# Background steps at even rates, the second block's tokens loaded at once, masks for two chunks, and last results further apart

## The chip, the cores and the metric

The kernel runs on one core of a Trainium2 chip. The time is device time of one launch in microseconds (us), as the median of several runs. A profile of one execution says when each engine worked: TensorE (PE, with its weight loads as PEld), VectorE (DVE), ScalarE (ACT), GpSimd (POOL) and SyncE (SP), which issues nearly all the transfers.

## The reference

One layer of a diffusion backbone in float32: 1024 latent tokens and 256 context tokens of 1024 channels, one sample. What is computed, cut short:

```
m = silu(c) @ w_ada + b_ada                 # 9 chunks of 1024: shift, scale, gate of three sublayers
h = x   + 0.5 * gate * rmsnorm(swiglu(modulate(rmsnorm(x)), w13_a, w2_a))     # latent, and so the context
p = modulate(rmsnorm(h)) @ w_in + b_in      # Fourier input, q, k, v, o, head gates, branch gates
h_l = bidirectional chunkwise mLSTM(q, k, v, gates; state from the context), 4 heads, 8 chunks of 128 tokens
  #   per chunk and direction: w = exp(dmat - m_t) where the triangle allows, s = (q k^T) * w
y = sigmoid(g_f) * (fft3(xf) @ w_four) + sigmoid(g_m) * (sigmoid(o) * rmsnorm(h_l) @ w_mproj)
h = h + gate * rmsnorm(y @ w_out)
out = h + 0.5 * gate * rmsnorm(swiglu(modulate(rmsnorm(h)), w13_b, w2_b))     # 22 row blocks of 128 in w2
```

## The kernel before

**Products.** Every float32 product of size is three matmuls (`mm3`, line 172): each operand is split into a rounded high part and the rest, and high x high, high x low and low x high are summed. So weights must be loaded (tile `wr`), cast by ScalarE to `wh`, and the difference taken by VectorE into `wl`, before TensorE can use them. `wunit` (lines 141 and 142) does that for a unit of 1024 columns; `split_act` (164 and 165) for others. There are three buffers each of `wr`, `wh` and `wl`. The large products over the 1024 latent tokens, seen as two blocks of 512, use Winograd's seven products of half-size blocks in place of eight: `ffn_in` and `mix_pairs` for the wide projections, `wino_out` for the two output products of the feed-forwards (order n = 1, 6, 7, 4, 5, 3, 2, with operands `gx` from memory; `done` adds and stores a finished column), `mix_values` for the values.

**Stages,** in order of time: modulation and the first block's normalisation; first feed-forward (`ffn_in`, then `wino_out` to 741 us); the context's feed-forward (`ffn_ctx_in`, `ffn_ctx_out`, to 930 us); head gates; the Fourier input's columns for block 1, then block 0 (`fourier_cols`, four units of weights each); pairs of q, k and gates (`mix_pairs`); values (`mix_values`); the context's projections and states; the mLSTM of four heads between projections of gates (1423 to 1789 us); the merge; second feed-forward, with its output product from 2454 us.

**Background work.** All work of other engines that isn't tied to the running product (normalisations, residuals, sums of blocks, modulation chunks, head steps) is written as generators that stop after each small step. Between the matmuls, `tick(part)` is called; it adds `rate * part` to a credit of at most 8 and runs one step for each whole credit. Credit that was left from before is spent at once. `later` appends generators and sets the rate; `drain` runs all that is left; `side` is a second such line of steps with its own rate:

```
        self.credit = min(self.credit + self.rate * part, 8.0)
        while self.bg and self.credit >= 1.0:
```

So rates and credit decide the order in which instructions stand in each engine's queue, and each queue runs in order. Nothing else orders the work; the tile framework adds the semaphores.

**Names that the change touches.** `load_x` loads tokens (tile `o` or `g`), squares them on ScalarE, transposes them and writes `xT`; for the second block it runs as a background generator, two row tiles at a step. `spill` writes the first block's tiles to `xT`. `second` makes the second block's operands. `enter` makes the operands of the mix, `combos` and `combos_rest` their sums over blocks. `mix_pairs` prepares weights of a pair in stages (`upto`): raw loads, sums on POOL, casts. `ada_rest` loads w_ada in tiles of 128 x 512 and sums them with the conditioning vector on VectorE (line 286), two loads ahead; in the mLSTM it is the side job, for chunks 5 to 8 of the modulation. In `mlstm_head`, `weigh` turns the log weights of a chunk into weights (adds a column and the mask on VectorE, exponential on ScalarE), and `scores` makes the products with q. `final` normalises and stores the last results, a column of 128 tokens at a time and a half of its 1024 channels; when the second half is there, its result is written.

Of the kernel before, what the change touches and what calls it, by code (L numbers as in the profile page):

```python
# [35 lines left out]
class Kernel:  # L36
# [349 lines left out]
    def load_x(self, src, T, name, out, keep=False, tag="o"):  # L386
# [6 lines left out]
        for j0 in range(0, n, 2):  # L393
            xs = {}
            for j in range(2):
                for hf in range(2):
                    x = xs[j, hf] = self.s512("g" if keep else tag)
                    r = (j0 + j) * P
                    nc.sync.dma_start(x, src[r : r + P, hf * TB : (hf + 1) * TB])
                    junk = self.s512("b" if tag == "o" else tag)  # L400
                    q = 2 * (j0 + j) + hf
                    nc.scalar.activation(junk, x, AF.Square, accum_out=ssq[:, q : q + 1])
                yield
# [73 lines left out]
    def operands(self, tiles, rstd, u, s, i, out):  # L477
# [10 lines left out]
        for k in range(4):  # L488
# [9 lines left out]
            nc.gpsimd.tensor_tensor(u1, uh[k].bitcast(F32), ul[k].bitcast(F32), op=ALU.add)  # L498
            nc.gpsimd.tensor_tensor(u2, uh[k + 4].bitcast(F32), ul[k + 4].bitcast(F32), op=ALU.add)
# [268 lines left out]
    def wino_out(self, w2, gx, tokens, done):  # L768
# [65 lines left out]
        for n in (1, 6, 7, 4, 5, 3, 2):  # L834
# [4 lines left out]
            for s in steps:  # L839
# [3 lines left out]
                if n == 2 and s[-1] in steps[-2]:  # L843
# [373 lines left out]
    def ctx_project(self, u, gw):  # L1217
# [46 lines left out]
        for c in range(2):  # L1264
# [4 lines left out]
            self.later(self.ctx_states((2 * c, 2 * c + 1), kt, va, gates), rate=3.0)  # L1269
# [122 lines left out]
    def mix_pairs(self, U, gates):  # L1392
# [29 lines left out]
        upto(0, "raw")  # L1422
        upto(0, 3)
# [116 lines left out]
    def mlstm_head(self, h, q, k, v, gates):  # L1540
# [50 lines left out]
        def weigh(c):  # L1591

            for d in range(2):
                nc.vector.scalar_tensor_tensor(W(c)[:, d, :], W(c)[:, d, :], col(3, c, d), self.mask[:, d, :],
                                               op0=ALU.add, op1=ALU.add)
            nc.scalar.activation(W(c), W(c), AF.Exp)

        def scores(c):
# [26 lines left out]
            nc.vector.tensor_scalar_mul(pr, SW[:, 1, :], rd[:, 1:2])
            nc.vector.scalar_tensor_tensor(pr, SW[:, 0, :], rd[:, 0:1], pr, op0=ALU.mult, op1=ALU.add)
# [62 lines left out]
    def fourier_cols(self, u2, b, units):  # L1689
# [459 lines left out]
```

## Time and profile before

| | us |
|---|---|
| median of 3 runs (2695.95 to 2700.22) | 2696.79 |
| the profiled execution | 2690.76 |
| its span in the trace | 2689.0 |
| TensorE busy | 2607.1 |
| VectorE busy | 1943.2 |
| ScalarE busy | 1157.7 |
| GpSimd busy | 248.7 |

The granted TensorE clock is 0.992 of full speed as a mean, and the transfers move 186 GB/s as a mean. The span runs from the first to the last instruction; the time holds 1.8 us more around it. Busy time of an engine is a sum over stages, so what limits a stage is read in windows of that stage. In a list of waits a row names who waited (engine, tile written, line), for what it waited last, and the total, number and longest of those waits.

### The profile page before, as it was taken

How to read it: one execution, taken by the hardware profiler on the slowest of the kernel's cores; microseconds unless marked ns; L12 is line 12 of the kernel's file. 1: busy time of each engine (PE TensorE's matmuls, PEld its weight loads, DVE VectorE, ACT ScalarE, POOL GpSimd, SP SyncE). 2: the span in 40 equal slices, each digit the busy share in tenths (PEclk: the TensorE clock that was granted, in tenths of full speed). 3: DMA queues.
4: the chain of work that ended last, by engine and by line, in shares of the span. 5: the costliest groups of instructions: out<-in, count | busy, mean ns of one | idle time of the engine just before them, and what ended most of it. 6: DMA issues, size and time to landing. Idle time of an engine off the chain costs nothing.

```text
span 2689.0 us, 34491 instructions
## 1 busy us (share of the span) xinstructions
PE 2607.1 (97%) x11497; PEld 2080.0 (77%) x11497; DVE 1943.2 (72%) x3493; ACT 1157.7 (43%) x2003; POOL 248.7 (9%) x380
## 2 busy tenths in 40 slices
PE   8999999999999999999999999999999999999998
PEld 5778888777777768887777777878887788888876
DVE  5688787899788748866856666656658787865665
ACT  4543333454455435542543443433345433334542
POOL 1111011000000023210000000000002010111000
PEclk9999999999999999999999999999999999999999
DMA  8765454868586642345665654456546554537774
GB/s 297 251 200 176 149 169 156 285 220 292 164 260 217 180 139 90 114 133 161 185 201 180 187 162 128 149 159 214 175 136 218 182 168 153 175 111 265 244 255 137
DMA packets 421978, 499.92 MB, mean 186 GB/s; under 512 B 27137, under 2 KB 258218, under 8 KB 421800
## 3 DMA queue, kind: packets, MB, share of 16 engines
q1 hardware_dynamic: 406728, 451.06, 53.7%
q0 software_dynamic: 14928, 46.59, 4.6%
q8 instruction: 91, 1.49, 0.2%
q14 instruction: 87, 0.71, 0.1%
q10 hardware_dynamic: 144, 0.07, 0.0%
HBM read 387.58 MB, written 110.04 MB: 185 GB/s over the span
## 4 chain that ended last, share of the span: by engine, by line
PE 74%; DVE 10%; DMA 8%; issue 5%; ACT 2%; SPq 1%; POOL 1%; DVEq 0%; POOLq 0%; ACTq 0%
PE mm L172 66%; DMA ld<-in_w_ada_dram 2%; DMA wr<-in_w_a_dram 2%; PE qc L1611 1%; DVE wl L142 1%; PE mm L1210 1%; DVE u L286 1%; DMA ld<-xT 1%; DMA ld<-h 1%; DVE b L441 1%; DMA t<-r_l 1%; PE aux L1762 1%; ACT wh L141 1%; PE mm L263 1%; DMA ld<-xT_c 0%
## 5 line engine op out<-in xcount | busy, mean ns | idle before, releaser
L172 PE MATMUL mm<-g,wh 128*128 128x512 f32 (+1 forms) x2112 | 686.8, 406 | 4.8 <-DVE m L1972 2.4
L172 PE MATMUL mm<-g,o 128*128 128x512 f32 x2352 | 555.9, 394 | 0.0
L172 PEld LDWEIGHTS mm<-g,o 128*128 128x128 f32 x2352 | 441.8, 188 | 103.9
L172 PEld LDWEIGHTS mm<-g,wh 128*128 128x128 f32 (+1 forms) x2112 | 389.9, 188 | 92.5 <-issue 3.8
L172 PE MATMUL mm<-g,wl 128*128 128x512 f32 (+1 forms) x1056 | 415.9, 395 | 0.0
L142 DVE TENSOR_TENSOR wl<-wr,wh 128x1024 fp32r<-128x1024 f32 x190 | 232.7, 1226 | 95.8 <-ACT wh L141 94.1
L172 PE MATMUL mm<-wh,g 128*128 128x512 f32 x920 | 295.3, 397 | 4.9 <-ACT wh L141 3.4
L141 ACT CAST wh<-wr 128x1024 fp32r<-128x1024 f32 x190 | 198.7, 1047 | 229.1 <-PE mm L172 164.8
L172 PE MATMUL mm<-u,wh 128*128 128x512 f32 (+1 forms) x848 | 268.3, 398 | 4.4 <-DVE m L518 2.8
L172 PEld LDWEIGHTS mm<-g,wl 128*128 128x128 f32 (+1 forms) x1056 | 198.6, 188 | 45.0 <-DVE wl L165 0.2
L172 PEld LDWEIGHTS mm<-wh,g 128*128 128x128 f32 x920 | 172.4, 188 | 47.9 <-ACT wh L141 4.7
L172 PE MATMUL mm<-wh,u 128*128 128x512 f32 x608 | 201.9, 406 | 3.9 <-ACT g L442 3.0
L172 PEld LDWEIGHTS mm<-u,wh 128*128 128x128 f32 (+1 forms) x848 | 159.8, 191 | 42.2 <-DVE m L518 3.2
L172 PE MATMUL mm<-wl,g 128*128 128x512 f32 x460 | 182.6, 397 | 0.2
L628 DVE TENSOR_TENSOR t<-mm,t 128x512 f32<-128x512 f32 x148 | 101.8, 688 | 99.6 <-PE mm L172 99.6
L172 PE MATMUL mm<-u,wl 128*128 128x512 f32 (+1 forms) x424 | 167.8, 398 | 2.5 <-DVE wl L142 2.5
L164 ACT CAST wh<-wr 128x1024 fp32r<-128x1024 f32 (+1 forms) x90 | 79.3, 881 | 165.2 <-PE mm L172 92.1
L164 ACT CAST o<-wa 128x512 fp32r<-128x512 f32 x108 | 66.9, 621 | 171.9 <-PE mm L172 165.4
L172 PEld LDWEIGHTS mm<-wh,u 128*128 128x128 f32 x608 | 116.3, 192 | 31.3 <-issue 3.4
L165 DVE TENSOR_TENSOR g<-t,g 128x512 fp32r<-128x512 f32 x156 | 104.5, 687 | 39.2 <-ACT g L164 31.9
L172 PE MATMUL mm<-wl,u 128*128 128x512 f32 x304 | 124.6, 410 | 6.0 <-DVE wl L142 6.0
L164 ACT CAST g<-t 128x512 fp32r<-128x512 f32 x156 | 92.5, 620 | 64.7 <-PE mm L172 46.4
(514 smaller groups left out, 3940.8 us busy)
## 6 DMA issues: line engine op xcount, KB each, us to landing
wr<-in_w_a_dram SPq DMA_DIRECT2D x124, 512.0 KB, 4.5
t<-gx SPq DMA_DIRECT2D x170, 256.0 KB, 4.0
wr<-in_w_b_dram SPq DMA_DIRECT2D x70, 512.0 KB, 4.4
wr<-in_w_in_dram SPq DMA_DIRECT2D x66, 512.0 KB, 4.0
gx<-m POOLq DMA_DIRECT2D x88, 256.0 KB, 3.7
gx<-t POOLq DMA_DIRECT2D x66, 256.0 KB, 3.8
ld<-in_w_ada_dram SPq DMA_DIRECT2D x64, 256.0 KB, 2.8
ld<-h SPq DMA_DIRECT2D x52, 256.0 KB, 3.7
```

The costliest lines, as they stand in the source:

```text
L141: nc.scalar.copy(hv, rv)
L142: nc.vector.tensor_tensor(lv, rv, hv.bitcast(F32), op=ALU.subtract)
L164: self.nc.scalar.copy(hi, src)
L165: self.nc.vector.tensor_tensor(lo, src, hi.bitcast(F32), op=ALU.subtract)
L172: mul = lambda x, y, start, stop: self.nc.tensor.matmul(out, x, y, start=start, stop=stop, skip_group_check=grown)
L263: nc.tensor.matmul(pt[:2, :], self.sc[:, k, :], t, start=k == 0, stop=k == ND - 1)
L286: nc.vector.scalar_tensor_tensor(acc[s], t, self.sc[:, k, s : s + 1], acc[s], op0=ALU.mult, op1=ALU.add)
L441: nc.vector.scalar_tensor_tensor(t, x, sc[:, d : d + 1], rb, op0=ALU.mult, op1=ALU.mult)
L628: add = lambda o, x, y: nc.vector.tensor_tensor(o, x, y, op=ALU.add)
L1210: nc.tensor.matmul(pt[:, :257], kw[:, i * P : (i + 1) * P], vaug, start=True, stop=True)
L1611: nc.tensor.matmul(pt[:, :257], at(q, i, c), C[:, i * 257 : (i + 1) * 257], start=i == 0, stop=i == 1)
L1762: nc.tensor.matmul(pt[:, jj * 256 : (jj + 1) * 256], zz[i][:, j * P : (j + 1) * P], m, start=i == 0, stop=i == 1)
```

## The change

It alters rates, resets credit, and moves instructions; the large products stay the same.

- `later` can set the credit to zero (`fresh`), and `paced` sets the rate when its generator begins.
- Second block's tokens: its loads use the 36 buffers of `g`, two row tiles (four loads) ahead; the first is issued before the feed-forward's weights. `spill` writes four tiles a step. The operands that follow have a rate of 2.8 in place of 5.
- `wino_out`: no background steps in the last three k of n = 5 and n = 3; for n = 2 with tokens as rows, the last three groups of k (and not two) are run together, column by column, so that a column ends every 15 matmuls in place of 9.
- `operands` (lines 498 and 499): the sums u1 and u2 of high and low parts go from POOL to VectorE, twice in each of its four steps' groups.
- `combos` at 0.6 without the credit from before (1.2), `enter` at 1.7 (2.0), and the context's states at 2.4 and then 10 (3), with no credit from before; the normalisations beside `mix_values` at 1.6 (2.0), the last feed-forward's operands at 4.2 (5.0).
- The first pair of `mix_pairs` is prepared at the last two units of `fourier_cols(0)`, not ahead of it.
- mLSTM: the mask is added to two chunks and both directions in one instruction; the column goes into the exponential as a bias, one for each direction; one of the two products of the scores goes to ScalarE. The side job has chunks 5 to 7 at 5.8 in place of 5 to 8 at 7.5.
- Chunk 8 is the side job in the last output product at 2.0, with tiles `u`; the row gains of `final` follow when it is done.

The diff, cut to its core:

```
     def later(self, *gens, rate=1.0, fresh=False):
         self.bg.extend(gens)
         self.rate = rate
+        if fresh:
+            self.credit = 0.0
+    def paced(self, gen, rate):
+        self.rate = rate
+        yield from gen
...
             u1, u2, s1 = self.s512("b"), self.s512("wa"), self.s512("b")
-            nc.gpsimd.tensor_tensor(u1, uh[k].bitcast(F32), ul[k].bitcast(F32), op=ALU.add)
-            nc.gpsimd.tensor_tensor(u2, uh[k + 4].bitcast(F32), ul[k + 4].bitcast(F32), op=ALU.add)
+            nc.vector.tensor_tensor(u1, uh[k].bitcast(F32), ul[k].bitcast(F32), op=ALU.add)
+            nc.vector.tensor_tensor(u2, uh[k + 4].bitcast(F32), ul[k + 4].bitcast(F32), op=ALU.add)
...
-                if n == 2 and s[-1] in steps[-2]:
+                if n == 2 and (s in steps[-3:-1] if tokens else s == steps[-2]):
                     continue
...
-                    self.tick(1 / 8)
+                    if n not in (5, 3) or k < NP - 3:
+                        self.tick(1 / 8)
...
+            if c % 2 == 0:
+                t = decay[c // 2].rearrange("p (d c s) -> p d c s", d=2, c=2)
+                nc.vector.tensor_tensor(t, t, self.mask.unsqueeze(2).to_broadcast([P, 2, 2, P]), op=ALU.add)
             for d in range(2):
-                nc.vector.scalar_tensor_tensor(W(c)[:, d, :], W(c)[:, d, :], col(3, c, d), self.mask[:, d, :],
-                                               op0=ALU.add, op1=ALU.add)
-            nc.scalar.activation(W(c), W(c), AF.Exp)
+                nc.scalar.activation(W(c)[:, d, :], W(c)[:, d, :], AF.Exp, bias=col(3, c, d))
...
-            nc.vector.tensor_scalar_mul(pr, SW[:, 1, :], rd[:, 1:2])
+            nc.scalar.activation(pr, SW[:, 1, :], AF.Copy, scale=rd[:, 1:2])
...
-            self.later(self.spill(xl[0][0], xl[0][2]), self.load_x(block(x, 1), TB, "1", xl[1]), second(), rate=5.0)
+            load = self.load_x(block(x, 1), TB, "1", xl[1], xtag="g")
+            next(load)
+            self.later(self.spill(xl[0][0], xl[0][2]), load, self.paced(second(), 2.8), rate=6.0)
...
-        self.later(enter(1), enter(0), rate=2.0)
+        self.later(enter(1), enter(0), rate=1.7)
...
-        self.later(self.combos(u2, U, held), rate=1.2)
+        self.later(self.paced(self.combos(u2, U, held), 0.6), rate=1.7)
...
-        next(pairs)
-        self.fourier_cols(u2, 0, units)
+        self.fourier_cols(u2, 0, units, lambda: next(pairs))
...
-                self.later(self.prenorm(self.reload(self.h1c, CTX), rc1, CTX, 1, 1, uc), rate=2.0)
+                self.later(self.prenorm(self.reload(self.h1c, CTX), rc1, CTX, 1, 1, uc), rate=1.6, fresh=True)
...
-        self.side, self.side_rate = self.ada_rest([0], [5, 6, 7, 8], ("ld", "acc", "rb", "b"), lag=2), 7.5
+        self.side, self.side_rate = self.ada_rest([0], [5, 6, 7], ("ld", "acc", "rb", "b"), lag=2), 5.8
...
+        self.side, self.side_rate = self.ada_rest([0], [8], "uuuu", lag=2), 2.0
         self.wino_out(w2, gx, True, self.final(h2t))
```

Four places show what moves in the queues. On VectorE, where the context's output product begins (L142 and L150 are the weight differences, L957 and L982 the context's own products, L1324 and L1352 the block sums of `combos`, L443 and L467 `enter`), before:

```order
L957 TENSOR_TENSOR t_7774<-mm_7680,t_7774 128x256
L1324 TENSOR_TENSOR t_7799<-g_7295,g_7303 128x512
L957 TENSOR_TENSOR t_7777<-mm_7681,t_7777 128x256
L1324 TENSOR_TENSOR ld_7801<-g_7299,g_7307 128x512
L1324 TENSOR_TENSOR ld_7803<-g_7468,g_7476 128x512
L142 TENSOR_TENSOR wl_7787<-wr_7784,wh_7786 128x1024
L165 TENSOR_TENSOR wa_7796<-aux_7790,wa_7795 128x512
L1324 TENSOR_TENSOR t_7805<-g_7472,g_7480 128x512
L1324 TENSOR_TENSOR b_7807<-t_7799,ld_7801 128x512
L1324 TENSOR_TENSOR t_7820<-g_7296,g_7304 128x512
L1324 TENSOR_TENSOR t_7799<-ld_7803,t_7799 128x512
```

and after, from the first block sum:

```order
L1352 TENSOR_TENSOR t_7871<-g_7517,g_7525 128x512
L467 SCALAR_TENSOR_TENSOR g_7705<-b_7779,ada_l,g_7697 128x512
L465 SCALAR_TENSOR_TENSOR b_7785<-ld_7759,pre_7540,rb_7717 128x512
L465 SCALAR_TENSOR_TENSOR b_7809<-ld_7783,pre_7540,rb_7717 128x512
L150 TENSOR_TENSOR wl_7860<-wr_7857,wh_7859 128x1024
L467 SCALAR_TENSOR_TENSOR g_7706<-b_7785,ada_l,g_7698 128x512
L150 TENSOR_TENSOR wl_7890<-wr_7887,wh_7889 128x1024
L467 SCALAR_TENSOR_TENSOR g_7707<-b_7809,ada_l,g_7699 128x512
```

The sums of `combos` stood several between two weight differences and now come later, with steps of `enter` in their place.

On SP, in `fourier_cols(0)` (the block's units are `wr` of 128x2x512, the first pair's weights `wr` of 128x8x128 and the tiles of L540 or L564; L1706 and L1736 store the results of the block before), before:

```order
L540 DMA ld_8654<-in_w_in_dram 128x4x128
L127 DMA wr_8619<-in_w_in_dram 128x8x128
L127 DMA wr_8667<-in_w_in_dram 128x2x512
L1706 DMA z_8434<-m_8598 128x512
L1706 DMA z_8434<-m_8603 128x512
L1706 DMA z_8434<-m_8608 128x512
L1693 DMA m_8659<-in_dft_dram 128x128
L1706 DMA z_8434<-m_8613 128x512
L127 DMA wr_8729<-in_w_in_dram 128x2x512
L127 DMA wr_8759<-in_w_in_dram 128x2x512
```

and after:

```order
L564 DMA ld_8784<-in_w_in_dram 128x4x128
L135 DMA wr_8708<-in_w_in_dram 128x2x512
L564 DMA b_8781<-in_w_in_dram 128x4x128
L564 DMA b_8782<-in_w_in_dram 128x4x128
L135 DMA wr_8715<-in_w_in_dram 128x8x128
L1736 DMA z_8361<-m_8591 128x512
L1736 DMA z_8361<-m_8596 128x512
L135 DMA wr_8717<-in_w_in_dram 128x8x128
```

The pair's `wr` stood ahead of three of the block's units and now stand behind its last.

On SP at the start of the feed-forward, behind the second block's tokens (`o` of L399, now `g` of L408), their transposes' stores to `xT` and the feed-forward's units `wr` (`wa` are partial sums reloaded), before:

```order
L127 DMA wr_847<-in_w_a_dram 128x4x128 x2
L127 DMA wr_930<-in_w_a_dram 128x4x128 x2
L127 DMA wr_1029<-in_w_a_dram 128x4x128 x2
L721 DMA wa_758<-p1s_319 128x512
L127 DMA wr_1099<-in_w_a_dram 128x4x128
L721 DMA wa_759<-p1s_319 128x512
L127 DMA wr_1099<-in_w_a_dram 128x4x128
L419 DMA xT_773<-o_809 128x2x256
```

and after:

```order
L408 DMA g_741<-in_x_dram 128x512
L408 DMA g_743<-in_x_dram 128x512
L442 DMA xT_707<-o_761 128x2x256
L442 DMA xT_707<-o_772 128x2x256
L135 DMA wr_836<-in_w_a_dram 128x4x128 x2
L442 DMA xT_707<-o_783 128x2x256
L442 DMA xT_707<-o_801 128x2x256
L745 DMA wa_832<-p1s_319 128x512
L135 DMA wr_939<-in_w_a_dram 128x4x128
```

The last tokens are loaded ahead of these units, and two stores of `xT` stand ahead of the first of them.

On SP in the last output product (L787 and L811 are its weights, L823 and L847 its operands, L1870 and L1900 reloads of `h2`, L285 the new loads of w_ada), after:

```order
L811 DMA g_21995<-in_w_b_dram 128x512
L811 DMA g_21999<-in_w_b_dram 128x512
L806 DMA wr_22129<-in_w_b_dram 128x512
L1900 DMA u_21901<-h_15999 128x512
L285 DMA u_21950<-in_w_ada_dram 128x512
L285 DMA u_21952<-in_w_ada_dram 128x512
L811 DMA g_22063<-in_w_b_dram 128x512
L811 DMA g_22067<-in_w_b_dram 128x512
L285 DMA u_21967<-in_w_ada_dram 128x512
L847 DMA t_22137<-gx_16000 128x512
```

where before stood

```order
L787 DMA g_22059<-in_w_b_dram 128x512
L787 DMA g_22063<-in_w_b_dram 128x512
L782 DMA wr_22181<-in_w_b_dram 128x512
L1870 DMA u_21917<-h_16095 128x512
L787 DMA g_22121<-in_w_b_dram 128x512
L787 DMA g_22125<-in_w_b_dram 128x512
L823 DMA t_22189<-gx_16096 128x512
```

Each new load stands a few rows ahead of the step on VectorE that uses it.

More of the change, by code (lines that the diff above doesn't have):

```diff
@@ L384, in sumsq, with load_x @@
         yield
-    def load_x(self, src, T, name, out, keep=False, tag="o"):
+    def load_x(self, src, T, name, out, keep=False, tag="o", xtag=None):
         nc = self.nc
@@ L392, in load_x, with load @@
         tiles = [self.slot("o")[:, :T] for _ in range(ND)] if keep else []
-        for j0 in range(0, n, 2):
+        def load(j0):
             xs = {}
@@ L396, in load_x, with squares @@
                 for hf in range(2):
-                    x = xs[j, hf] = self.s512("g" if keep else tag)
+                    x = xs[j, hf] = self.s512(xtag or ("g" if keep else tag))
                     r = (j0 + j) * P
                     nc.sync.dma_start(x, src[r : r + P, hf * TB : (hf + 1) * TB])
[L400 to L403, printed above, removed]
+            return xs
+        def squares(j0, xs):
+            for (j, hf), x in xs.items():
+                junk = self.s512("b" if tag == "o" else tag)
+                q = 2 * (j0 + j) + hf
+                nc.scalar.activation(junk, x, AF.Square, accum_out=ssq[:, q : q + 1])
+        ahead = None
+        if xtag:
+            ahead = load(0)
+            yield
+        for j0 in range(0, n, 2):
+            xs = ahead if xtag else load(j0)
+            if xtag:
+                ahead = load(j0 + 2) if j0 + 2 < n else None
+            squares(j0, xs)
+            yield
             for d0 in range(0, ND, 2):
@@ L1051, in tok_major @@
             ww = next(units)
+            if late is not None and k0 >= ND - 4:
+                late()
             for kk in range(2):
@@ L1268, in ctx_project @@
                 self.drain()
-            self.later(self.ctx_states((2 * c, 2 * c + 1), kt, va, gates), rate=3.0)
+            self.later(self.ctx_states((2 * c, 2 * c + 1), kt, va, gates), rate=(2.4, 10.0)[c], fresh=True)
         self.m0 = gates[3]
@@ L1422, in mix_pairs @@
         upto(0, "raw")
+        yield
         upto(0, 3)
@@ L1683, in mlstm_head, with fourier_cols @@
             yield
-    def fourier_cols(self, u2, b, units):
+    def fourier_cols(self, u2, b, units, late=None):
         nc = self.nc
@@ L1886, in final @@
         nc = self.nc
-        sg = self.gain(0, 2)
         rows = []
-        for h in range(2):
-            pt = self.rows_bcast(sg[:, 4 * h : 4 * h + 4], 4)
-            rows.append(self.s512("rb"))
-            nc.scalar.copy(rows[h], pt)
         parts = {}
@@ L1896, in half @@
         def half(b, h, d, t, acc):
+            if not rows:
+                for _ in self.side:
+                    pass
+                self.side = None
+                sg = self.gain(0, 2)
+                for i in range(2):
+                    pt = self.rows_bcast(sg[:, 4 * i : 4 * i + 4], 4)
+                    rows.append(self.s512("rb"))
+                    nc.scalar.copy(rows[i], pt)
             if acc is not None:
@@ L2088, in run @@
             else:
-                self.later(self.operands(self.reload(self.h2, TB, TB), r2[1], u, 0, 2, U), rate=5.0)
+                self.later(self.operands(self.reload(self.h2, TB, TB), r2[1], u, 0, 2, U), rate=4.2)
         w13, w2 = a["w13_b"][0], a["w2_b"][0]
```

15 lines of the change are left out of this document (8 added, 7 removed).

## The prediction

> **What bounds the kernel now.** I read the page's totals first, then a table of stages (busy time of each engine between borders that I set at the stages' matmuls), then the chain's sharp end: what TensorE itself waited for.
>
> ```profile
> span 2689.0 us, 34491 instructions
> PE 2607.1 (97%) x11497; PEld 2080.0 (77%) x11497; DVE 1943.2 (72%) x3493; ACT 1157.7 (43%) x2003; POOL 248.7 (9%) x380
> ```
>
> TensorE is busy for 2607.1 of 2689.0 us. The change leaves its work as it is (10,727 instructions in the order against 10,726), so all it can win or lose is in the other 81.9 us, and in the clock. The stage rows give, after the stage's length, the busy time of PE, its weight loads, DVE, ACT and POOL, then the granted clock, the DMA share and GB/s. Length less PE is the idle time of the stage.
>
> ```profile
> 66.00:125.00 59.00, 54.21 (x251) 43.49 (x250) 34.61 (x61) 31.20 (x55) 9.05 (x10) 0.97 0.87 273
> 125.00:177.00 52.00, 47.83 (x199) 37.94 (x198) 49.64 (x68) 28.48 (x45) 9.51 (x9) 0.97 0.67 208
> 527.00:675.00 148.00, 141.65 (x617) 110.82 (x618) 140.05 (x224) 75.05 (x127) 0.00 (x0) 1.00 0.79 260
> 845.00:885.00 40.00, 33.60 (x136) 24.62 (x135) 39.17 (x57) 21.00 (x29) 0.54 (x1) 0.96 0.51 165
> 970.00:1002.00 32.00, 28.36 (x108) 19.34 (x106) 12.27 (x12) 7.83 (x12) 5.21 (x4) 1.00 0.41 118
> 1196.00:1423.00 227.00, 218.99 (x978) 170.80 (x977) 151.76 (x335) 93.70 (x153) 13.64 (x60) 1.00 0.60 181
> 1423.00:1789.00 366.00, 347.47 (x1649) 281.59 (x1648) 244.56 (x811) 155.18 (x389) 20.63 (x40) 0.98 0.54 163
> 2047.00:2440.00 393.00, 390.55 (x1686) 316.63 (x1687) 299.15 (x455) 146.97 (x239) 49.65 (x76) 1.00 0.49 157
> 2440.00:2678.00 238.00, 236.53 (x1056) 190.59 (x1054) 153.11 (x229) 111.82 (x199) 20.32 (x28) 1.00 0.71 240
> ```
>
> VectorE is nearly full in just the places where TensorE idles (39.17 of 40 us at 845, 49.64 of 52 at 125, 140.05 of 148 at 527), though over the span it has 28% left: bursts of background work, not a full engine. TensorE's own waits name them (total, times, longest):
>
> ```profile
> PE mm L172 <- DVE wl L142: 8.5, 9, 3.3
> PE aux L1650 <- ACT m L1633: 5.0, 3, 2.4
> PE aux L1632 <- DVE ada_l L314: 3.9, 1, 3.9
> PE aux L410 <- DMA o<-in_x_dram: 3.8, 1, 3.8
> PE mm L172 <- ACT wh L141: 3.4, 3, 1.2
> PE mm L172 <- ACT g L442: 3.0, 1, 3.0
> PE mm L172 <- DVE m L518: 2.8, 1, 2.8
> PE qc L1611 <- DVE m L1626: 2.5, 1, 2.5
> PE mm L172 <- DVE m L1972: 2.4, 2, 1.8
> ```
>
> A wait also costs clock afterwards. In four-microsecond slices, around the 2.8 us wait (136) and the 3.3 us wait (872):
>
> ```profile
> 136.00:140.00 4.00, 2.78 (x7) 1.97 (x8) 4.00 (x4) 0.00 (x0) 2.55 (x2) 0.74 0.56 183
> 140.00:144.00 4.00, 4.00 (x16) 3.21 (x15) 4.00 (x7) 1.84 (x3) 0.00 (x0) 0.83 0.82 243
> 872.00:876.00 4.00, 0.95 (x3) 0.76 (x4) 4.00 (x7) 0.51 (x1) 0.00 (x0) 0.90 0.00 0
> 876.00:880.00 4.00, 3.85 (x12) 2.78 (x11) 4.00 (x7) 2.19 (x3) 0.00 (x0) 0.67 0.43 131
> ```
>
> The slices after them ran 7 to 16 matmuls at clocks of 0.67 to 0.83; 4 x (0.26 + 0.17) and 4 x (0.10 + 0.33) make 1.7 us lost after each. The Trainium skill (TensorE: Matmul & The Clock Gate, Part 1) puts the drop after an idle window of about 3.4 us; here 2.8 us was enough once. By the page's bound neither wait would cost clock and my sum would be 3 us smaller; the measurement decides.
>
> **The change part by part**, against the profiled execution's 2690.76 us, which stands 6.0 under the median of 2696.79; the same difference is taken from the median. Gains are positive.
>
> *Start (66 to 125 us): -1, bounds -7.6 to +4.8.* The x loads of the second block now go out before the first feed-forward's weights, so the 3.8 us wait for `o<-in_x_dram` goes. But the weights of two units, loaded ahead of the block's transposes until now, stand on SP behind the writes of `xT`, which wait for ScalarE's copies; these follow eight tiles' squares on ScalarE. A late unit costs about what the x wait costs, 3.8, and there are two. Between two late units and all of the stage's idle time (4.8) I take -1, next to the x wait traded for one late unit.
>
> *Operands of the second block (125 to 177): +4.5, bounds 2 to 5.7.* Idle 4.17, clock 0.03 x 52 = 1.6. Rate 5 becomes 2.8, and VectorE, full now, gets the time until matmul 420 instead of 363. What is late next is the operands' use at the pairs, at 177 us, and they end before it.
>
> *First output product (527 to 675): +1.5, bounds 0 to 4.* Ticks are held back in the last three k of n=5 and 3, so the sums L1972 no longer queue behind background steps; of their 2.4 us I take 1.5. The steps held back run a few us later. *Entering the mix (741 to 815): +0.5, bounds -1 to 2:* 2.0 becomes 1.7 and the queue's order stays.
>
> *Combos (845 to 885): +7.5, bounds 4 to 8.1.* Credit of 8 lets 16 steps run within 96 matmuls. VectorE has these groups there:
>
> ```profile
> L142 DVE TENSOR_TENSOR wl<-wr,wh 128x1024 fp32r<-128x1024 f32 x14 | 16.9, 1220 | 2.5 <-ACT wh L141 2.5
> L1324 DVE TENSOR_TENSOR t<-g,g 128x512 f32<-128x512 f32 x7 | 4.8, 683 | 0.0
> ```
>
> and each weight difference L142 that TensorE needs waits behind several 0.68 us additions. At rate 0.6 and no credit they spread over 246 matmuls, a step every 3.5 us and not every 1.4. Idle 6.4 and clock 1.7 make 8.1; part stays since `enter` still runs there. The steps left over go to the next 300 matmuls, where VectorE's sum of work per 48 matmuls (11.1 us), by these durations, comes to 10.6 to 11.6 us instead of 5.6 to 8.3: covered, just.
>
> *First columns of the Fourier block (970 to 1002): +3.2, bounds 1.2 to 3.6.* The first pair's raw loads and casts held two of three `wr` and `wh`, and the block's units came one at a time: three waits for `wh L141`, 3.4 us. The pair now comes at the last two units. Late next would be the pair's own sums on POOL, before the first pair product.
>
> *Second block's values (1196 to 1423): +2.5, bounds 0 to 3.0.* The one wait for `g L442` came when a normalisation step waiting for its load stood on VectorE ahead of n=4's sums; 1.6 and no credit set it apart. The stage's other 5 us of idle time I leave.
>
> *mLSTM (1423 to 1789): +6.5, bounds -2 to 13.* The side job:
>
> ```profile
> DVE acc L286 <- DMA ld<-in_w_ada_dram: 22.0, 21, 3.2
> DVE t L1594 <- DMA t<-r_l: 15.5, 6, 3.6
> L1594 DVE SCALAR_TENSOR_TENSOR t<-t,cols_l,mask x64: 328/346/352, 1432.1 to 1679.0; 128x128 f32<-128x128 f32 x64
> L286 DVE SCALAR_TENSOR_TENSOR acc<-ld,sc,acc x56: 742/751/755, 1425.8 to 1714.8; 128x512 f32<-128x512 f32 x56
> L1625 DVE TENSOR_SCALAR m<-t,den x32: 278/280/285, 1453.3 to 1766.6; 128x128 f32<-128x128 f32 x32
> L1596 ACT ACTIVATE t<-t x32: 408/417/431, 1432.7 to 1679.4; 128x256 f32<-128x256 f32 x32
> L1654 ACT ACTIVATE m<-aux,cc 128x128 f32<-128x128 f32 x64 | 20.3, 362 | 12.2 <-PE aux L1650 12.1
> ```
>
> VectorE loses 64 masks x 0.346 = 22.1, 32 products x 0.280 = 9.0 and 16 ada steps x 0.751 = 12.0, and gains 16 masks of two chunks, at 0.683 as the addition of the same 512 columns: 10.9. Net -32 of 244.56 us. ScalarE gains 64 exponentials and 32 products at about 0.36 (the 128x128 row) less 32 x 0.417: +21 on 155.18. VectorE stood blocked 22.0 us for ada loads; 48 loads at a rate of 5.8 instead of 64 at 7.5 leave each 7.5/5.8 = 1.3 times as long to land. Of 18.5 us idle, 7.8 (L314, L1633 in part, L1626) stand behind that queue; 6.5 is most of them, with nothing for the clock. If ScalarE is late instead, the gain is gone: the lower bound. The loads of `r_l` wait as before.
>
> *Entering the second feed-forward (2047 to 2440): -0.5, bounds -2.5 to 1.5.* 16 sums of 0.68 us go from POOL to VectorE, which is 76% full there.
>
> *Last output product (2440 to 2678): -2.5, bounds -8 to 0.* Sixteen ada loads and steps now run here:
>
> ```profile
> 2454.00:2537.00 83.00, 82.94 (x388) 67.20 (x387) 59.78 (x96) 49.90 (x93) 12.59 (x18) 1.00 0.90 315
> 2460.00:2480.00 20.00, 20.00 (x94) 16.19 (x93) 14.30 (x23) 10.85 (x22) 3.30 (x5) 1.00 1.04 386
> t<-gx SPq DMA_DIRECT2D x42, 256.0 KB, 4.2
> g<-in_w_b_dram SPq DMA_DIRECT2D x16, 256.0 KB, 6.7
> ```
>
> TensorE hardly waits now. The sixteen loads are 4.2 MB, 51 GB/s over 83 us; 315 + 51 = 366 is under the 386 seen at 2460, so no time is put on the bytes. But each step stands on VectorE 9 to 15 matmuls (2 to 3.5 us) behind its load in the order, landing takes 4.2 to 6.7, and VectorE waits out the difference with weight splits behind it. VectorE's work over matmuls 9174 to 9372 (45.6 us) becomes 46.7 us from 34.8. I take 2.5 of that as not covered.
>
> *Tail (from 2678): +1.8, bounds 1 to 2.5.* The last columns, now 15 matmuls (3.5 us) apart and not 9 (2.1):
>
> ```profile
> 2677.77 0.40 PE L172 MATMUL mm<-wh,g 128*128 128x512 f32 x1
> 2684.31 1.42 DVE L1915 SCALAR_TENSOR_TENSOR u<-u,rs_r,u 128x512 f32<-128x512 f32 x2 [0.73 <-POOL rs_r L346]
> ```
>
> 7.6 us pass from the last matmul's end to the last result. A column takes VectorE 0.69 + 0.69 + 1.42 and 0.3 of small work, 3.1: at 2.1 apart a backlog of about 2 us builds, at 3.5 none.
>
> **Sum:** -1 + 4.5 + 1.5 + 0.5 + 7.5 + 3.2 + 2.5 + 6.5 - 0.5 - 2.5 + 1.8 = 24.0. That is 2666.8 for a profiled execution, and 2696.8 - 24.0 = 2672.8 as the median.
>
> **The rivals.**
> *The mLSTM gives nothing* (chance 0.20): the waits for `r_l` and ScalarE's 21 us take the place of the ada loads; the term goes to its lower bound of -2. 2681. For it: the longest list of waits on ScalarE is there already (L1633). Against: VectorE's net loss of 32 us.
> *Weights late at the start* (0.13): both units late, 7.6 us. 2679. For it: SP writes `xT` ahead of them. Against: the stage has DMA share left (0.87).
> *Work only moved* (0.08): VectorE's smoothed load, 10.6 to 11.6 of 11.1, tips over in the combos' new place and before the value products; the 15.2 us of combos, operands and Fourier columns come back as waits, and the mLSTM gives 1 of its 6.5. 2693, no change. For it: VectorE is at 39.17 of 40 us there now, and no work is taken from it. Against: before the burst and behind it stand slices with 5 to 8 us of 11.1.
> *Slower* (0.06): in the last product VectorE waits at each of sixteen ada steps as long as the longest in the mLSTM (3.2 us), 51 us with splits queued behind. Without its -2.5 the sum is +26.5, so it decides from 1.7 us a step; at 3.2 the time is 2721. Against: the mLSTM's mean is 22.0 / 64 = 0.34.
> *Memory bound there* (0.03): 366 GB/s above what is sustained, 0.64 MB late, 2 us: 2675. The Trainium skill (DMA: Bandwidth & Descriptors, Where 436 GB/s comes from) gives about 358 GB/s from HBM to one core; the 386 at 2460, not all of it from HBM, disagrees.
>
> **How the numbers follow.** The forecast has 0.50: 2673, by itself 2660 to 2685. The half-widths of the bounds, added in squares, give about 11 us. The first two rivals take the upper side to 2689 with a few us of their own; the lower side, 2657, is a mLSTM and a start near their upper bounds. Left out are the work only moved, the slower rival and a few tails. 0.2% (5.4 us) is about what can be told from no change: faster 0.50 + 0.20 + 0.13 + 0.03 = 0.86, same 0.08, slower 0.06.
>
> **What would show it.** In the profile after, around the combos (845 to 885 now) no wait of 3 us for a weight difference and a clock of 1.00; three `wh` waits gone at 970; the ada waits of VectorE under 15 us in the mLSTM with ScalarE no longer than 1 us late; 2440 to 2678 with PE idle under 5 us; last result under 6 us after the last matmul; and from 66 to 125 us idle time for weights instead of x. I am wrong if VectorE's new steady load is late by itself, or if the weights at the start or in the last product come late by more than a landing time.

## The result, and the profile after

The changed kernel takes 2665.48 us (median of 4 runs, 2660.61 to 2667.17) against 2696.37 before (4 runs, 2693.86 to 2700.22): a ratio of 0.9881, 95% interval 0.9864 to 0.9899. The forecast was 2673, range 2657 to 2689. The profiled execution of the changed kernel took 2665.76, at its median; that of before, 2690.76, lay 5.6 under its median. So the two traces below differ by 25.0 us, next to the forecast's sum of 24.0, and the medians by 30.9.

The page's totals:

```profile
span 2664.0 us, 34450 instructions
PE 2595.7 (97%) x11497; PEld 2075.6 (78%) x11497; DVE 1929.2 (72%) x3429; ACT 1173.2 (44%) x2067; POOL 222.3 (8%) x364
```

TensorE idles 68.3 us in place of 81.9 and, with the same number of matmuls, is busy 11.4 us less: nearly half of the gain is not idle time but faster matmuls. (In a second execution, shown below as "again", it was 8.4 of 28.2 us.) Some stages, in windows moved to the same matmuls (columns as in the prediction):

```profile
66.50:131.00 64.50, 56.79 (x250) 44.80 (x250) 45.08 (x78) 35.57 (x63) 3.90 (x6) 0.95 0.84 260
131.00:177.20 46.20, 45.70 (x198) 36.91 (x197) 39.29 (x58) 22.57 (x35) 2.70 (x5) 1.00 0.67 210
177.20:211.50 34.30, 32.17 (x132) 25.66 (x131) 23.57 (x40) 12.28 (x25) 3.83 (x6) 0.95 0.54 163
849.50:880.30 30.80, 30.80 (x145) 25.18 (x144) 28.06 (x40) 19.55 (x26) 0.61 (x1) 1.00 0.80 254
887.00:928.00 41.00, 39.03 (x169) 31.25 (x168) 40.17 (x58) 21.49 (x27) 1.31 (x2) 1.00 0.62 196
967.90:993.70 25.80, 25.80 (x106) 19.35 (x106) 11.87 (x14) 7.84 (x13) 12.83 (x10) 1.00 0.40 112
1410.50:1763.00 352.50, 339.41 (x1639) 276.00 (x1638) 221.13 (x712) 167.21 (x449) 20.58 (x40) 1.00 0.52 157
2425.70:2561.00 135.30, 133.77 (x614) 107.27 (x613) 101.48 (x156) 76.70 (x136) 13.98 (x20) 1.00 0.88 302
```

These are the start, the second operands, the pairs' start, the old place of the combos (845 to 885 before), the 41 us from 887, the first pair, the mLSTM, and the first 528 matmuls of the last product, which before were

```profile
2454.20:2583.90 129.70, 129.64 (x587) 104.58 (x586) 87.82 (x132) 71.96 (x128) 12.57 (x17) 1.00 0.82 277
```

The idle time of the second operands, of the combos' old place and of the first pair is gone. But the start idles 7.7 us (4.8 before), the pairs' start has a new 2.1, the last product 1.5, and behind the combos' old place, where the sums now run, VectorE is full (40.17 of 41 us) and TensorE idles 2.0. Among TensorE's waits:

```profile
PE mm L180 <- DVE wl L150: 10.3, 7, 2.3
PE mm L180 <- ACT wh L172: 4.1, 2, 2.4
PE aux L1680 <- ACT m L1663: 3.7, 4, 1.7
PE mm L180 <- DVE m L2008: 3.1, 1, 3.1
PE mm L180 <- ACT t L649: 2.1, 1, 2.1
```

The waits for `ada_l`, `wh` of the first pair and the tokens of the second block have left the list. Weight differences still lead it, with more in total (10.3, was 8.5) but a shorter longest wait (2.3, was 3.3). L649 is new, and L2008 (L1972 before) is longer.

A finer comparison uses the large products' matmuls, 9888 in each trace, as mile posts: the time from the start of one to that of a later one. "Again" is a second profiled execution of the changed kernel.

| stage (matmuls) | before | after | again | gain | forecast |
|---|---|---|---|---|---|
| start (0 to 332) | 94.3 | 100.5 | 98.6 | -6.2, -4.3 | -1.0 |
| second operands (332 to 528) | 51.8 | 46.0 | 46.4 | 5.8, 5.4 | 4.5 |
| first pair of the feed-forward (528 to 660) | 30.6 | 34.5 | 31.6 | -3.9, -1.0 | 0 |
| first output product (1848 to 2772) | 232.3 | 237.2 | 234.9 | -4.9, -2.6 | 1.5 |
| context, entering (2772 to 3248) | 129.6 | 125.4 | 125.1 | 4.2, 4.5 | 0.5 |
| combos (3248 to 3564) | 84.9 | 78.7 | 80.0 | 6.2, 4.9 | 7.5 |
| head gates, Fourier columns (3564 to 3804) | 71.8 | 65.5 | 65.4 | 6.2, 6.4 | 3.2 |
| values, context's projections (4644 to 5388) | 227.1 | 222.4 | 225.5 | 4.7, 1.6 | 2.5 |
| mLSTM (5388 to 6156) | 366.1 | 352.5 | 352.0 | 13.6, 14.1 | 6.5 |
| second feed-forward in (7116 to 8964) | 439.5 | 436.9 | 436.9 | 2.7, 2.6 | -0.5 |
| last output product (8964 to 9887) | 223.5 | 229.2 | 227.7 | -5.7, -4.2 | -2.5 |

### The profile page after: what moved, and what is told of

Same layout as the page of the kernel before. It is cut to its first block, busy times and chain, and to the rows that moved or that the text cites. A ratio compares the mean times of both kernels' runs of the same rounds, so it can differ in the third digit from the quotient of the medians.

```text
span 2664.0 us, 34450 instructions
## 1 busy us (share of the span) xinstructions
PE 2595.7 (97%) x11497; PEld 2075.6 (78%) x11497; DVE 1929.2 (72%) x3429; ACT 1173.2 (44%) x2067; POOL 222.3 (8%) x364
## 4 chain that ended last, share of the span: by engine, by line
PE 73%; DMA 10%; DVE 10%; issue 4%; ACT 2%; SPq 1%; POOL 0%; DVEq 0%; POOLq 0%; ACTq 0%
PE mm L180 66%; DMA wr<-in_w_a_dram 2%; DVE wl L150 2%; DMA ld<-in_w_ada_dram 1%; PE qc L1641 1%; PE mm L1238 1%; DMA ld<-xT 1%; DMA ld<-h 1%; DMA g<-in_w_ada_dram 1%; DVE u L294 1%; DMA t<-r_l 1%; PE aux L1792 1%; ACT wh L149 1%; DVE g L173 1%; DMA wa<-p1s 0%
## 5 line engine op out<-in xcount | busy, mean ns | idle before, releaser
L150 DVE TENSOR_TENSOR wl<-wr,wh 128x1024 fp32r<-128x1024 f32 x190 | 233.1, 1228 | 94.1 <-ACT wh L149 93.9
L180 PE MATMUL mm<-wh,u 128*128 128x512 f32 x608 | 199.5, 400 | 0.0
L173 DVE TENSOR_TENSOR wl<-wr,wh 128x1024 fp32r<-128x1024 f32 (+1 forms) x90 | 91.2, 1014 | 33.3 <-ACT wh L172 33.3
```

The lines of the kernel that those rows point to most:

```text
L150: nc.vector.tensor_tensor(lv, rv, hv.bitcast(F32), op=ALU.subtract)
L173: self.nc.vector.tensor_tensor(lo, src, hi.bitcast(F32), op=ALU.subtract)
L180: mul = lambda x, y, start, stop: self.nc.tensor.matmul(out, x, y, start=start, stop=stop, skip_group_check=grown)
```

## The experiments

Each was timed beside runs of the kernel before, whose median lay between 2691 and 2700 us from one group of experiments to the next; so the ratios compare across groups, and the times alone don't. Single parts were also read from one trace each by the mile posts. Some stages that an edit doesn't touch come back within 0.3 us (660 to 1848, 3804 to 4644). Others scatter by 1 to 5 us: the start, and what begins at 528, 1848, 2376, 2772, 4644, 4980 and 7116. The mLSTM took 363.9 to 367.5 in three kernels with its old form, and 351.2 to 353.8 in seven with its new one.

**The scores' new form alone** (before, with the mask for two chunks, the biased exponential and the product on ScalarE; the diff is the one shown under the change).

> The kernel before with one part of the change: the mask added for two chunks, the exponential with a bias, one product of the scores on ScalarE; the side job keeps chunks 5 to 8 at 7.5. My theory: VectorE's work in the mLSTM holds TensorE there, so this part (20 us less on VectorE) brings about half of the 13.5 us that the mLSTM (matmuls 5388 to 6156) gained, 5 to 7 us, and the whole kernel is 5 to 7 us faster. Rival: the ada loads alone hold TensorE (through VectorE's waits for them); then the mLSTM gains at most 1.5 us, and ScalarE's 21 us more may cost 1 or 2.

2697.5 us, ratio 1.0003 (0.9988 to 1.0018). The mLSTM took 366.2 us, before 366.1. The rival's number; my theory falls: VectorE's load fell and nothing came of it. By its busy time the load fell by 12.5 us (244.5 to 232.0), not by the 20 that I had added up from single durations.

**The ada loads alone.**

```
-        self.side, ... = self.ada_rest([0], [5, 6, 7, 8], ...), 7.5
+        self.side, ... = self.ada_rest([0], [5, 6, 7], ...), 5.8
...
+        self.side, ... = self.ada_rest([0], [8], "uuuu", lag=2), 2.0     # in the last output product
```

The row gains of `final` go behind chunk 8 here too, as in the changed kernel.

> The kernel before with chunk 8 of the modulation moved from the mLSTM (48 loads at 5.8) to the last output product (16 loads at 2.0), and nothing else. My theory: 5 to 7 us gained in the mLSTM, 4 to 6 us lost over matmuls 8964 to 9492, in all 0 to 3 us faster. Rival 1 (the ada loads alone hold TensorE in the mLSTM): 12 us gained there, in all 6 to 8 us faster. Rival 2 (the last product's loss comes from its other changes): no loss over 8964 to 9492, in all 5 to 7 us faster.

Ratio 0.9976 (0.9961 to 0.9992). The mLSTM took 350.5 us, 15.6 less; the last product 228.5, 5.0 more. Rival 1 has the mLSTM right: the loads (fewer of them, and at a slower rate) carry all of that gain. Its total (6 to 8 us, ratio 0.9970 to 0.9978) fits too; rival 2 has the same total but no loss at 8964 to 9492, where 4.8 us were lost.

**Rates of enter and combos alone** (1.7, and 0.6 from their beginning).

> The kernel before with only the rates of enter (1.7) and combos (0.6, set when they begin). My theory: matmuls 2772 to 3564 take 8 to 11 us less, and up to 2 us of it come back by matmul 3804; 7 to 10 us faster in all. Rival (work only moved): what is won up to 3564 is lost again by 3804, under 3 us in all.

Ratio 0.9991 (0.9971 to 1.0010). Stage 2772 to 3564 took 207.7 us, 6.7 less, under my 8 to 11. The rival's total was met (2.4 us by the ratio), but not for its reason: 3564 to 3804 took 71.7 us, as before, so nothing was lost again there. 5.0 of the 6.7 lie ahead of the sums, at 2772 to 3248 (124.6), where enter works at its slower rate; 3300 to 3396, where the burst stood, took 29.4 and not less than before's 29.0. The place of the sums explains it: in the trace enter's last step stands at matmul 3336 (3288 before, 3420 in the changed kernel), and 17 of the 32 sums start before matmul 3408 (29 before, 1 in the changed kernel).

**The changed kernel again.**

> The changed kernel once more, to see which differences of single stages stand. My theory: all are set by the order in the queues, so the losses of 3.9 us at matmuls 528 to 660 and of 3.8 us at 1848 to 2112, and the gain of 13.5 us in the mLSTM, come back within 1 us. Rival: those two losses are chance of the transfers in one execution, and come back at under 1.5 us.

2665.6 us, ratio 0.9888 (0.9861 to 0.9914). The mLSTM's gain came back at 14.1; the losses at 528 and at 1848 to 2112 came back at 1.0 and 1.6 in place of 3.9 and 3.8. At 528 most of the 3.9 belongs to one execution (later runs with the new start took 31.7 to 32.7 us there). The wait for L649 was 2.1 us in the first and this in the second:

```profile
PE mm L180 <- ACT t L649: 0.4, 1, 0.4
```

Both traces show what L649 stands behind on ScalarE: the square of a context token tile whose load is late, here in the first execution (4.13 us idle there in the second, 1.5 before):

```profile
183.80 0.63 ACT L415 ACTIVATE u<-u 128x512 f32<-128x512 f32 x1 [4.80 <-DMA u<-in_ctx_dram]
```

At 1848 to 2112 the other kernels with the change took 68.2 to 69.6 us (before 66.1), so up to 3.5 us stay; but that stage scatters without the change too (69.0 in the run with the ada loads alone).

**Ticks not held back in `wino_out`.**

```
-                    if n not in (5, 3) or k < NP - 3:
-                        self.tick(1 / 8)
+                    self.tick(1 / 8)
```

> The changed kernel with background steps allowed again in the last k of n = 5 and n = 3 of wino_out. The order shows that this also lets enter end 60 matmuls earlier, so that 18 of the 32 block sums of combos stand before matmul 3408 (in the changed kernel 2). My theory, that the place of these sums and not their rate makes the gain: matmuls 2376 to 2772 take 1 to 2 us less than in the changed kernel, 3300 to 3396 take 4 to 6 us more, 3396 to 3564 take 2 to 3 less; in all 1 to 4 us slower than the changed kernel. Rival (the rate of 0.6 is what counts): 3300 to 3396 stays within 1.5 us of the changed kernel's 23.6, and the whole is 0 to 2 us faster.

2669.9 us, ratio 0.9919 (0.9901 to 0.9938). The 96 matmuls from 3300 took 27.9 us (changed: 23.6), and those to 3564 2.3 less, as my theory had it; 3248 to 3564 took 85.4 (changed: 78.7 and 80.0; before: 84.9). So with all rates kept, what the held ticks put off, the sums above all, carries the whole gain there. By the ratios the whole is 8 to 10 us slower than the changed kernel, more than my 1 to 4, though the interval overlaps with that of its second run. 2376 to 2772 as a whole stayed as in the changed kernel (102.6 us, 102.2), against my 1 to 2. The windows of those 96 matmuls, first before:

```profile
862.00:891.00 29.00, 25.10 (x102) 19.26 (x101) 28.79 (x44) 13.00 (x17) 0.00 (x0) 0.94 0.49 157
```

then with the ticks not held back:

```profile
867.20:895.10 27.90, 25.18 (x102) 19.23 (x101) 27.00 (x38) 13.24 (x17) 0.54 (x1) 0.94 0.58 191
```

and in the changed kernel:

```profile
863.30:887.00 23.70, 23.09 (x102) 18.40 (x101) 20.97 (x29) 14.13 (x19) 0.61 (x1) 1.00 0.79 257
```

In the two windows with VectorE full TensorE idles 3.9 and 2.7 us at a clock of 0.94; with 20.97 of 23.7 it idles 0.6 at 1.00. The clock need not fall: at 887 to 928 above VectorE is full too, and it stays at 1.00. Matmuls 2640 to 2772 took 31.7 us as before the change, against 33.3 with the ticks held: holding them back cost 1.6 there, and its use lay elsewhere, in delaying what follows.

**The place of the sums, without the rest of the change** (before, with enter at 1.4 and combos at 0.6).

```
-        self.later(enter(1), enter(0), rate=2.0)
+        self.later(enter(1), enter(0), rate=1.4)
-        self.later(self.combos(u2, U, held), rate=1.2)
+        self.later(self.paced(self.combos(u2, U, held), 0.6), rate=1.4)
```

> The kernel before with enter at 1.4 and combos at 0.6, so that the block sums stand where they stand in the changed kernel (1 before matmul 3408, not 29), and nothing else. My theory (their place makes the gain): matmuls 3300 to 3396 take 23.5 us and not 29.0, 3396 to 3564 take 1.5 to 3 us more, 2772 to 3300 take 3 to 7 us less; 6 to 10 us faster in all. Rival (what lies ahead, residual and held ticks, is needed too): 3300 to 3396 stays above 27 us.

2683.9 us, ratio 0.9946 (0.9926 to 0.9966). 3300 to 3396 took 23.6 us, and 2772 to 3564 took 202.8, 11.6 less than before:

```profile
852.70:876.30 23.60, 23.60 (x110) 19.22 (x109) 21.01 (x29) 14.67 (x19) 0.61 (x1) 1.00 0.82 268
```

Over these 96 matmuls the place of the sums is enough. But it isn't the cause of all 11.6 us: 9.7 lie ahead of the sums, at 2772 to 3248 (119.9 for 129.6), where the edit slows enter. Behind the 96 matmuls, 3396 to 3564 took 43.7, 4.7 more than before (I had said 1.5 to 3), so over 3248 to 3564 only 2.0 are left. What is moved comes back in part, and slowing enter is a gain of its own. By the ratio the whole gained 14.6 us (9 to 20), over my 6 to 10.

**The first pair ahead of the Fourier columns again.**

```
+        next(pairs)
+        next(pairs)
-        self.fourier_cols(u2, 0, units, lambda: next(pairs))
+        self.fourier_cols(u2, 0, units)
```

> The changed kernel with the first pair prepared ahead of fourier_cols(0), as before. My theory: matmuls 3564 to 3804 take 71.7 us again and not 65.5, the three waits for wh are back, 6 us slower than the changed kernel. Rival (the gain there came from the combos' place, not from the pair): at most 2 us slower.

2666.4 us, ratio 0.9906 (0.9891 to 0.9921; the kernel before took 2691.2 on that chip): 5 to 7 us slower than the changed kernel by the ratios, with intervals that overlap. 3564 to 3804 took 71.0 us, 5.5 more than in the changed kernel, and the waits were back. The window of matmuls 3708 to 3804:

```profile
958.80:991.40 32.60, 29.02 (x113) 19.84 (x111) 12.79 (x13) 8.05 (x13) 7.10 (x6) 1.00 0.40 120
```

and TensorE's waits in it:

```profile
PE mm L180 <- ACT wh L149: 3.4, 3, 1.1
```

**Chunk 8 beside the merge.**

```
-        self.side, ... = self.ada_rest([0], [8], "uuuu", lag=2), 2.0      # in the last output product
+        self.side, ... = self.ada_rest([0], [8], "gggg", lag=2), 1.0      # from the merge on
```

> The changed kernel with chunk 8 of the modulation as a side job of the merge (rate 1.0, tiles g) in place of the last output product. My theory: the 5.7 us lost over matmuls 8964 to 9492 come back whole, and the merge (6156 to 7116), where TensorE idles 1 us of 258, loses under 1: 4 to 6 us faster than the changed kernel. Rival (16 loads cost the same wherever they stand, as VectorE waits for them): the merge loses 3 to 6 us, no gain.

2659.7 us (2657.4 to 2661.3), ratio 0.9879 (0.9865 to 0.9894): not told apart from the changed kernel's 0.9881 and 0.9888. (It is the lowest time of all variants, but the kernel before was 5 us faster on that chip too.) The last product took 225.2 us, 4.0 and 2.5 less than in the two traces of the changed kernel; 9360 to 9492 stayed at 32.5 (before 30.8). The merge took 1.9 more. Its windows, last product and merge:

```profile
2423.70:2555.00 131.30, 131.30 (x602) 106.51 (x601) 90.00 (x135) 73.79 (x132) 13.97 (x20) 1.00 0.82 278
1757.90:1985.60 227.70, 227.16 (x1005) 184.68 (x1004) 148.05 (x200) 86.59 (x120) 2.35 (x2) 1.00 0.59 189
```

and in the merge the side job's matmuls (line, duration, first and last start):

```profile
L305 PE MATMUL aux<-g,sel x4: 387/395/398, 1826.3 to 1913.3; 128*2 128x512 f32 x4
L318 PE MATMUL aux<-ident,g x8: 196/196/218, 1843.4 to 1930.4; 2*128 2x2 f32 x8
```

TensorE idles 0.5 us in the merge, so the 1.9 us is its own work: a chunk brings four matmuls of 512 columns and eight small transposes. In the last product that work was 2.5 us (133.77 us busy for 131.30). In the first trace 1.5 us of idle time came on top; in the second there was none:

```profile
2424.00:2557.80 133.80, 133.79 (x615) 107.23 (x613) 101.58 (x156) 76.66 (x136) 13.98 (x20) 1.00 0.89 305
```

So this part costs about the same wherever it stands, and waits came on top in one execution of two. Neither theory's number holds for the whole.

**The start of before.**

```
-            load = self.load_x(block(x, 1), TB, "1", xl[1], xtag="g")
-            next(load)
-            self.later(self.spill(...), load, self.paced(second(), 2.8), rate=6.0)
+            self.later(self.spill(...), self.load_x(block(x, 1), TB, "1", xl[1]), second(), rate=5.0)
```

> The changed kernel with the start of before: tokens of the second block in pairs from the tiles o, spill a tile at a step, the second block's operands at rate 5. My theory, from two traces of the changed kernel (0 to 528: -0.4 and +1.1 us against before): the two halves cancel, matmuls 0 to 528 within 1.5 us of the changed kernel. Rival (weights late at the start hide a gain of the even operands): 0 to 288 at least 2 us faster and 288 to 528 at least 2 us slower. The losses at 528 to 660 (3.9, then 1.0) go in either if they hang on the start's order, and stay if not.

2664.8 us, ratio 0.9904 (0.9887 to 0.9920). 0 to 288 took 4.4 and 2.6 us less than in the two traces of the changed kernel, 288 to 528 7.4 and 7.1 more: the rival's signs. With the border at matmul 332, where the second operands begin, 0 to 332 took 92.1 (changed: 100.5 and 98.6) and 332 to 528 57.4 (46.0 and 46.4). So the new start costs 6 to 8 us ahead of the second operands and pays 11 in them. 528 to 660 took 30.7, so the loss there hangs on the new start. The whole (0 to 660: 180.2 against 181.0 and 176.6 in two executions of the changed kernel) doesn't tell the two starts apart.

**The mLSTM's 48 loads at the old rate** (7.5 in place of 5.8).

> The changed kernel with its 48 ada loads in the mLSTM at the old rate of 7.5, so the same loads with the old lead over their use. My theory (the lead is what counts: VectorE's waits for the loads, 22.0 us before, 13 to 14 now): these waits rise to 20 us or more and matmuls 5388 to 6156 take 5 to 8 us more than the changed kernel's 352. Rival 1 (the number of loads counts): the stage stays within 2 us, as the last quarter of it then has no side job. Rival 2 (only TensorE's own work for chunk 8, about 2 us, and its waits count): the same within 2 us with VectorE's waits up.

2668.8 us, ratio 0.9893 (0.9861 to 0.9924). The mLSTM took 359.4 us, 6.9 more; VectorE's waits rose less than I had expected. Its window:

```profile
1409.90:1769.30 359.40, 341.34 (x1639) 278.94 (x1638) 221.77 (x712) 169.29 (x449) 19.00 (x40) 0.99 0.52 154
```

VectorE's waits for transfers there:

```profile
DVE t L1624 <- DMA t<-r_l: 18.2, 9, 3.8
DVE acc L294 <- DMA ld<-in_w_ada_dram: 16.7, 15, 3.4
```

and in the changed kernel:

```profile
DVE t L1624 <- DMA t<-r_l: 14.7, 10, 3.3
DVE acc L294 <- DMA ld<-in_w_ada_dram: 14.1, 17, 2.1
```

Idle time is 18.1 us again (before 18.5, changed 13.1). So the spacing of the loads carries the idle time; it shows in the longest wait for one (3.4, not 2.1) more than in their sum. What this stage still gains on before, 6.7 us, is TensorE's busy time (347.47 to 341.34).

**The operands' sums on POOL again** (two lines in `operands`).

> The changed kernel with u1 and u2 of the operands on POOL again. My theory (they make the second block's first operands late, and with 8 x 0.69 x 2 us on VectorE move 3 to 4 us to the pairs' start): 528 to 660 takes 30.6 us as before and not 31.6 to 34.5, 288 to 528 is the same within 1 us, 7116 to 8232 up to 2 us more (POOL's 2.6 us sum on the chain there); in all within 2 us of the changed kernel. Rival (the loss at 528 comes from the slower rate of 2.8): 528 to 660 stays above 31.5.

2675.8 us, ratio 0.9919 (0.9890 to 0.9948). 528 to 660 took 31.8, so the loss there isn't the sums' (the rival); 0 to 528 took 150.8 (changed: 146.4, 145.0) and 7116 to 7500 took 103.6 (96.4, 96.5). My "within 2 us" was wrong: by the ratios the whole is 8 to 10 us slower than the changed kernel, so VectorE seems to do better by these sums. The stages alone don't show it: 7116 to 7500 scatters from 96.4 to 100.2 with the sums on either engine.

**Four edits together:** chunk 8 beside the merge, no ticks held with enter at 1.45, the scores as before.

> The changed kernel with four edits that the runs point to: chunk 8 as the side job of the merge; ticks no longer held back in wino_out, with enter at 1.45 so that the block sums stay late; the scores of the mLSTM as before (mask and product on VectorE). My theory, from single stages: 5.5 us from chunk 8 and the merge, 1.6 at 2640 to 2772, 1 to 2 in the mLSTM; 2656 to 2659 us where the changed kernel has 2665. Rival (the scores' new form is needed with the slower side job): the mLSTM takes 3 us more, and the whole is no faster than with chunk 8 moved alone (2659.7).

2663.0 us, ratio 0.9876 (0.9845 to 0.9907), not told apart from the changed kernel. 2640 to 2772 took 31.7 and 2772 to 3564 took 199.5, as hoped; the mLSTM took 355.9, 3.4 more than the changed kernel, as the rival said, though the same stage with the old scores took 350.5 with the ada loads alone moved. What the scores' form is worth stays open between these two.

## Why the prediction was right or wrong

**The sum was right, and by luck: its terms weren't.** Forecast 24.0, measured 25.0 between the two traces. That it came so close is errors that cancel: in the first trace the terms over their forecast (the mLSTM above all) are 21 us over, and those under it (the first output product and the start above all) 20 us under. The medians differ by 5.9 more because I took the before's 6 us between profiled execution and median to hold for both; it didn't.

- *Combos:* right in kind, and 6.2 and 4.9 of the 7.5. In the old place of the burst 9.3 us were won (matmuls 3248 to 3371: 40.1 us, then 30.8). "Covered, just" was too hopeful: 3371 to 3564 took 3.1 and 4.4 more, where VectorE is now full. My words "at rate 0.6 and no credit" name the smaller cause: the run with those rates alone left the 96 matmuls at 29.4. The diff also resets no credit at `combos`, though the text on the change says so.
- *Entering the mix:* 4.2 and 4.5 for 0.5, over my upper bound of 2. I had looked at the queue's order there, which stays; the slower rate alone gave 5.0 in the run with the rates of enter and combos, and 9.7 at a rate of 1.4.
- *Fourier columns, values:* right, the first too small. The pair is worth 5.5 (forecast 3.2). I counted idle time alone: over 3564 to 3804 it fell from 4.3 to 0.1 us, but TensorE's busy time fell by another 2.0, at a recorded clock of 1.00 in both; why these matmuls became faster stays open. The values' first 192 matmuls took 45.2 us in every kernel with the change and 46.9 to 50.4 without.
- *mLSTM:* right sign, half the size. I named two steps. That VectorE loses 32 us of work carried nothing: its scores alone gave 0.1, and by busy time the whole loss was 23.3 (244.46 to 221.13). That fewer loads with a longer lead unblock VectorE was right, and gave it all. Of 13.6, 5.4 is idle time (18.5 to 13.1), about 2 is TensorE's own work for chunk 8, which I had left out, and the remaining 6 is clock: 347.47 us busy became 339.41, at a granted clock of 0.98 and then 1.00. I had written "with nothing for the clock".
- *Last product:* right sign, too small by 2 to 3, and by another cause than I named. Chunk 8 costs 2.5 to 4.0, near my 2.5, but that is luck: 2.5 of it is TensorE's own matmuls, which I had left out, and the queue on VectorE, which I priced alone, is the 1.5 us of waits in one execution of two. Another 1.7 is the row gains' broadcast, moved here from ahead of the product; 1.3 shows as a gain at 8232 to 8964. The bytes show no limit: 302 and 305 GB/s over the window, and no idle time in the second execution. The Trainium skill (DMA: Bandwidth & Descriptors, Where 436 GB/s comes from) gives about 358 GB/s from HBM to one core. The window stays under that.
- *Start:* wrong in size, -6.2 and -4.3 for -1, though inside my bound of -7.6. The x wait went, as forecast, but in its place TensorE waited, from matmul 128, 4.4 and 3.7 us for weight differences and 2.3 for the row sums `rx`; in the before these were nothing and 1.0. Whether the weights' loads or VectorE's queue made the differences late isn't shown.
- *Second operands:* right, 5.8 and 5.4 for 4.5. The idle time of 4.17 us became 0.5, and the clock went from 0.97 to 1.00. "They end before it" holds as far as TensorE's waits show, but the pairs' start still lost 1.0 to 3.9, to which I had given nothing: the first drained result (L649) stands on ScalarE behind the late context tokens.
- *First output product:* wrong sign. Of 4.9 and 2.6 us, 1.6 is the held ticks at 2640 to 2772, and 3.8 and 1.6 fell at 1848 to 2112, which the edit doesn't touch and which scatters. The four sums L2008 wait no longer behind new background steps, but behind operand splits and a step already standing there, and take 2.5 us by themselves:

```profile
655.20 0.48 DVE L465 SCALAR_TENSOR_TENSOR b<-ld,pre,rb 128x256 f32<-128x256 f32 x1 [0.85 <-DMA ld<-xT_c]
655.60 1.29 DVE L173 TENSOR_TENSOR g<-t,g 128x512 fp32r<-128x512 f32 x2
656.80 2.48 DVE L2008 TENSOR_TENSOR m<-mm,m 128x512 f32<-128x512 f32 x4
```

- *Second feed-forward in:* 2.7 for -0.5. At 7500 to 8232 1.4 came with every kernel whose operands run at 4.2, with sums on POOL too; VectorE's 16 sums cost nothing. The other 1.3 is the row gains' broadcast.
- *Tail:* from the last matmul's start to the span's end 11.2 us became 9.1; 2.1 for 1.8.

Of the rivals, "the mLSTM gives nothing" was wrong in its number; what the prediction held against it, VectorE's 32 us, carried nothing, and the loads did. "Weights late at the start" came true in part, for about the price of one late unit. "Work only moved" describes 3 to 4 us behind the combos. "Slower" named a place that does lose, 4.2 to 5.7 us and not 51.

## What to carry to other kernels

Before VectorE's load is cut, look at what its queue waits for: here sixteen fewer loads at a gentler rate gave 15.6 us in their stage, and a load 12.5 us lighter gave none. A burst of background work is cured by where it stands in the queue, and rates are a blunt way to put it there: check the place, and count what comes back behind it. When a job is moved, price the bound engine's own part of it first; it is the part that no place hides.

## What the runs showed beyond that

In some stages with waits of 2 to 4 us the matmuls themselves were slower: the granted clock was 0.94 in the 29 us of the combos and 0.98 over the mLSTM's 366 us, and 1.00 with the waits shorter. In the trace the clock falls to 0.5 for 3.41 us at a time, which costs 1.7 us, as here in the mLSTM before:

```profile
1472.60:1476.00 3.40, 3.40 (x10) 2.66 (x9) 2.85 (x12) 0.80 (x3) 0.77 (x1) 0.50 0.50 146
```

Up to the last matmul this happened 11 times in the trace before, four of them in the mLSTM, 5 times in the first of the changed kernel, and 6 times (two of them 6.83 us long) in the second. Summed, that makes about 10 of TensorE's 11.4 us, and 5 of the 8.4. Not each wait brings it: with the rates of enter and combos alone, the 96 matmuls had 5.1 us of waits, and the clock stayed at 1.00; in the trace before, a wait of 2.5 us that ended at 1471.3 brought it and one of 3.0 us that ended at 1245.3 didn't. The fall that the prediction laid to a wait of 2.8 us came after that wait and another of 1.0.

Also, the text on the kernel said that nothing but rates and credit orders the work; the order of the changed kernel shows otherwise: the block sum of `t_7871` stands ahead of steps whose tiles were made earlier (`b_7785`, `g_7706`), so it seems that the framework moves single instructions forward as well.
